# Second-product pairs moved beside the last column tiles of the first product in a fused encoder's feed-forward blocks

## The chip, the cores and the metric

The kernel runs on one core of one Trainium2 chip, as one launch. The metric is the device time of one execution in microseconds (us); lower is better. All times below are of that core.

## The reference

Two layers, each with a feed-forward block, a mixer (two kinds of attention) and a second feed-forward block, on 256 tokens of width 1024, all in float32:

```python
for l in range(DEPTH):                                   # DEPTH = 2
    x = layer_norm(ALPHA * x + 0.5 * swiglu(x, ffn1_w_in[l], ffn1_w_out[l]), ...)
    mix = hybrid_mixer(x, ...)
    x = layer_norm(ALPHA * x + mix, ...)
    x = layer_norm(ALPHA * x + 0.5 * swiglu(x, ffn2_w_in[l], ffn2_w_out[l]), ...)

def swiglu(x, w_in, w_out):                              # w_in 1024 x 5632, w_out 2816 x 1024
    gate, up = split(x @ w_in)
    return (silu(gate) * up) @ w_out
```

The mixer is untouched by the change; the four feed-forward blocks are all changed in the same way. They are called here by layer and place: 00, 02, 10, 12 (12 is the last).

## The kernel before, in words

Every float32 operand is split into a rounded high half (type fp32r) and the rest, and a product is three fp32r products. So each 128-row piece of a weight matrix is loaded by SyncE into a `raw` tile (128x1024, 512 KB; five buffers), ScalarE casts it into a high half `wh` (L118, for pairs L72), and VectorE subtracts to get the low half `wl` (L119, for pairs L73). `wh` and `wl` have nine buffers each. TensorE's order is the order of the code; the order on the other engines is set by a scheduler with priorities when the program is built (weight work has a low one), and each engine then runs its list strictly in that order.

A feed-forward block has 22 column tiles of the hidden width (index j, 128 wide). Tiles 0 to 3 are made by `first`. For tile 4 on, `col` makes for a tile two accumulations, `hg` (gate) and `hu` (up), each in one of the eight PSUM banks: eight matmuls of 512 columns with `wh` (L419, `wide`) and eight of 256 with `wl` (L424, `narrow`). `col` takes two tiles j, j+1 at a time (the first two singly), so four banks are in use and the other four rest; the order of wide and narrow alternates (`flip`). ScalarE then copies half of a bank to `tl` (L434), VectorE adds the other half (L435), ScalarE applies Silu (L436), VectorE multiplies (L438), and the result is split into high and low halves in a tile `g` (L441, L442). A g tile holds two column tiles, so its index is q = j/2.

The second product multiplies g (22 pieces of 128 of the inner dimension, index k) with `w_out`. A single piece ("o", `step`, L503) costs 12 matmuls of 512 columns for the two token halves t = 0, 1. Six couples of pieces (q = 3 to 8, the tuple STR) use a Strassen-like scheme instead (`pair`, L527): seven products of three matmuls, 21 where two singles take 24. For this VectorE makes four sums of blocks of g (`sums`, L457 to L460, with their halves at L461 and L462) and four sums of blocks of the two raw weight pieces (`_make_pair`, L86 to L89), whose halves come out as three full `wh`/`wl` tiles and one half tile `t4` (index b, t, a, f in the tile names). Lookahead for weights is counted in slots, nine in all; a pair counts four.

The order in a block: all 22 column tiles; then, by PLAN, `o o S o S S S S S` (o a single, S a pair); then the pair accumulators in four extra banks (`pp`) are folded into x by VectorE (L540 to L549); then seven more singles (TAIL) for t = 0, layer norm of t = 0, the same seven for t = 1 with the transposes of the normed t = 0 (`to_xt`, L327) put three half-steps ahead of the end, and layer norm of t = 1. Norm weights (`lng`, `lnb`) have a tile each of their own and are loaded in `col`'s loop.

Of the kernel before, what the change touches and what calls it, by code (L numbers as in the profile page):

```python
# [33 lines left out]
TAIL = 7  # L34
# [6 lines left out]
STR = (3, 4, 5, 6, 7, 8)  # L41
PLAN = "o o S o S S S S S"
# [17 lines left out]
class Weights:  # L60
# [6 lines left out]
    def _halves(self, i, raw, nm=""):  # L67
        nc = self.nc
        n = raw.shape[-1]
        wh = self.pool.tile([P, 1024], F32R, tag="wh", name=f"wh{i}{nm}", bufs=9)  # L70
        wl = self.pool.tile([P, 1024], F32R, tag="wl", name=f"wl{i}{nm}", bufs=9)
        nc.scalar.copy(wh[:, 0:n], raw)  # L72
        nc.vector.tensor_tensor(wl[:, 0:n], raw, wh[:, 0:n].bitcast(F32), ALU.subtract)  # L73
        return [tuple(w[:, c : c + 512] for w in (wh, wl)) for c in range(0, n, 512)]
# [21 lines left out]
    def _slots(self, i):  # L96
        return 4 if self.srcs[i][0] == "S" else 1

    def _make(self, i):
# [4 lines left out]
        wh = self.pool.tile([P, 1024], F32R, tag="wh", name=f"wh{i}", bufs=9)  # L104
        wl = self.pool.tile([P, 1024], F32R, tag="wl", name=f"wl{i}", bufs=9)
# [30 lines left out]
def encoder_kernel(  # L136
# [36 lines left out]

    singles = [k for k in range(JT) if k // 2 not in STR]
    singles, tail = singles[: len(singles) - TAIL], singles[len(singles) - TAIL :]
    plan, left, pairs = [], list(singles), list(STR)
    for u in PLAN.split():
        plan.append((u, (left if u == "o" else pairs).pop(0)))
    assert not left and not pairs

    def out_rows(w):
        row = lambda k: w[k * P : (k + 1) * P, :]
        rows = [row(k) if u == "o" else ("S", row(2 * k), row(2 * k + 1)) for u, k in plan]
        return rows + [row(k) for k in tail]

    srcs = []
    for l in range(DEPTH):
        srcs += [f1_b[l, k] for k in range(KT)]
        srcs += [f1_in[l, j, s] for j in range(JT - NB) for s in range(2)]
        srcs += out_rows(f1_out[l])  # L190
# [8 lines left out]
        srcs += [f2_b[l, k] for k in range(KT)]  # L199
        srcs += [f2_in[l, j, s] for j in range(JT - NB) for s in range(2)]  # L200
        srcs += out_rows(f2_out[l])
# [111 lines left out]
    def load_gb(l, n):  # L313
        gt = wp.tile([P, D], F32, tag="lng", name=f"lng{l}{n}")
        nc.sync.dma_start(gt, ln_g[l, n].partition_broadcast(P))
        bt = wp.tile([P, D], F32, tag="lnb", name=f"lnb{l}{n}")
        nc.sync.dma_start(bt, ln_b[l, n].partition_broadcast(P))
        return gt, bt
# [42 lines left out]
    def ffn(l, n, last=False):  # L361
        nonlocal wi
        nm = f"{l}{n}"
        gs = [gp.tile([P, 2, 2, SEQ], F32R, tag="g", name=f"g_{nm}_{q}") for q in range(JT // 2)]
# [29 lines left out]
        def first_t(gv, t):  # L394
# [3 lines left out]
            for q in range(2):  # L398
                a = slice(t * P, (t + 1) * P)
                dh = gs[q][:, :, 0, a]  # L400
                nc.scalar.copy(dh, tr[:, 2 * q : 2 * q + 2, :])
                dv.tensor_tensor(gs[q][:, :, 1, a], tr[:, 2 * q : 2 * q + 2, :], dh.bitcast(F32), ALU.subtract)

        def col(*js, flip=False):
# [3 lines left out]
            for j in js:  # L408

                hs = [ps.tile([P, 2, SEQ], F32, tag="b", name=f"h{'gu'[s]}_{nm}_{j}") for s in range(2)]  # L410
                tl = tp.tile([P, 2, SEQ], F32, tag="tl", name=f"tl_{nm}_{j}", bufs=2)
# [3 lines left out]

            def wide(hs, ws, s):
                for k in range(KT):

                    mm(hs[s], ws[s][0][:, k * P : (k + 1) * P], xx[:, k], start=(k == 0 and not flip),  # L419
                       stop=(k == KT - 1 and flip), skip_group_check=flip)  # L420

            def narrow(hs, ws, s):
                for k in range(KT):
                    mm(hs[s][:, 1, :], ws[s][1][:, k * P : (k + 1) * P], xx[:, k, 0], start=(k == 0 and flip),  # L424
                       stop=(k == KT - 1 and not flip), skip_group_check=flip)

            one, two = (narrow, wide) if flip else (wide, narrow)
            for j, hs, tl, ws in ts:
                for s in range(2):
                    one(hs, ws, s)  # L430
            for j, hs, tl, ws in ts:
                for s in range(2):
                    two(hs, ws, s)
                    nc.scalar.copy(tl[:, s], hs[s][:, 1, :])  # L434
                    dv.tensor_tensor(tl[:, s], hs[s][:, 0, :], tl[:, s], ALU.add)  # L435
                nc.scalar.activation(tl[:, 0], tl[:, 0], AF.Silu)  # L436
                gv = tl[:, 1]
                dv.tensor_tensor(gv, tl[:, 0], gv, ALU.mult)  # L438
                q, jj = divmod(j, 2)
                n = P if q in STR and jj == 0 else SEQ  # L440
                nc.scalar.copy(gs[q][:, jj, 0, 0:n], gv[:, 0:n])  # L441
                dv.tensor_tensor(gs[q][:, jj, 1, 0:n], gv[:, 0:n], gs[q][:, jj, 0, 0:n].bitcast(F32), ALU.subtract)  # L442
                if q in STR and jj:
                    sums(q, ts[0][2][:, 1], gv)

        sm = {}

        def sums(q, g0, g1):

            f = tp.tile([P, 4, P], F32, tag="tmp", name=f"sf_{nm}_{q}")  # L450
            if STR.index(q) < 3:
                s = xp.tile([P, 2, 4, P], F32R, tag="x", name=f"s_{nm}_{q}")
                sh, sl = s[:, 0], s[:, 1]
            else:
                sh, sl = (tp.tile([P, 4, P], F32R, tag="tmp", name=f"s{c}_{nm}_{q}") for c in "hl")
# [22 lines left out]
        for j in (NB + 1, *range(NB + 2, JT, 2)):  # L478

            col(*((j,) if j == NB + 1 else (j, j + 1)), flip=(j % 4 == 0 or j == NB + 1))  # L480
# [3 lines left out]
            if j == JT - 6:  # L484
                gb = load_gb(l, n)
                if n == 0:
                    load_mix(l)

        k0, k1 = singles[0], tail[-1]
        kl = tail[-SPLIT]  # L490
        acc = [[(slice(512 * h, 512 * h + 512), ps.tile([P, 512], F32, tag="b", name=f"acc_{nm}_{t}{h}"),
                 k0, tail[-SPLIT - 1] if last and t and h else k1) for h in range(2)] for t in range(2)]
# [12 lines left out]
        pp = {}  # L505

        def pair(q, w, first, final):
            b11, b21, b22, t4, t1, t2, t3 = w
            if first:
                for c in (5, 7, 1, 6):  # L510
                    pp[c] = ps.tile([P, 512], F32, tag="b", name=f"pp_{nm}_{c}")
            sh, sl = sm[q]
            blk = lambda kk, t: [gs[q][:, kk, e, t * P : (t + 1) * P] for e in range(2)]
            smb = lambda c: (sh[:, c], sl[:, c])
            s1, s2, s3, s4 = (smb(c) for c in range(4))
            for o, (ah, al), (bh, bl) in (
                (acc[0][0][1], blk(1, 0), b21),
                (acc[0][1][1], s4, b22),
                (pp[5], s1, t1),
                (pp[7], s3, t3),  # L520
                (pp[1], blk(0, 0), b11),
                (pp[6], s2, t2),
                (acc[1][0][1], blk(1, 1), t4),
            ):
                own = any(o is p for p in pp.values())
                for e, (g, ww) in enumerate(((ah, bh), (ah, bl), (al, bh))):
                    mm(o, g, ww, start=(own and first and e == 0), stop=(own and final and e == 2))  # L527

# [453 lines left out]
```

## Time and profile before

| | us |
|---|---|
| median of 3 runs (lowest, highest) | 929.22 (928.66, 930.1) |
| the profiled execution, its own time | 929.28 |
| its span, first to last instruction | 927.5 |
| TensorE busy in the span | 919.1 |
| VectorE busy | 804.9 |
| ScalarE busy | 577.8 |
| block 10 from start to end (463.1 to 643.0) | 179.9 |

In profile rows PE is TensorE's matmuls, PEld its weight loads, DVE VectorE, ACT ScalarE, POOL GpSimd, SPq SyncE's queue, and L12 is line 12 of the kernel. A busy TensorE says little by itself, since matmuls overlap and their ends are modelled: what counts is the spacing of their starts. For VectorE and ScalarE too, a row's duration is longer than the spacing of two such instructions behind one another. A timeline row merges neighbours of one kind; its figures are start and duration, and in brackets stands how long the engine idled ahead of it and what ended that.

### The profile page before, as it was taken

To read this page: it belongs to the slowest core of one execution; us is meant where nothing else is said; L and a number is where in the kernel's file an instruction comes from. 1 tells how busy PE (TensorE), PEld (TensorE's weight loads), DVE (VectorE), ACT (ScalarE), POOL (GpSimd) and SP (SyncE) were. 2 spreads that over 40 slices of the span, in tenths; PEclk is the share of its full clock that TensorE was granted. 3 is DMA by queue.
4 is the path that set the end of the run, shared out by engine and by line. 5 is a ranking of instruction groups with operands and counts; after the bars stand their busy time and mean duration, and the time that the engine had idled before them with its cause. 6 is when DMAs were issued, how large, how long until landed. Compare 5 with 4: busy or idle time off the path is not lost.

```text
span 927.5 us, 13795 instructions
## 1 busy us (share of the span) xinstructions
PE 919.1 (99%) x4958; PEld 784.9 (85%) x4958; DVE 804.9 (87%) x1388; ACT 577.8 (62%) x982; POOL 17.0 (2%) x27
## 2 busy tenths in 40 slices
PE   9999999999999999999999999999999999999996
PEld 6888888888878888888888888888888888888885
DVE  7898899998987677899986888999988876888997
ACT  5768656546865666656646666664478656666660
POOL 0000000000000000000000000000000000000000
PEclk9999999999999999999999999999999999999998
DMA  8976445774426755545775665466844365665451
GB/s 320 313 265 203 160 137 191 246 260 154 128 90 206 248 182 182 159 136 191 257 262 196 187 192 168 136 231 208 290 112 137 100 236 188 189 192 163 136 205 46
DMA packets 51380, 176.30 MB, mean 190 GB/s; under 512 B 6512, under 2 KB 8304, under 8 KB 51312
## 3 DMA queue, kind: packets, MB, share of 16 engines
q1 hardware_dynamic: 51024, 175.03, 58.0%
q8 instruction: 39, 0.64, 0.3%
q10 hardware_dynamic: 288, 0.39, 0.1%
q14 instruction: 29, 0.24, 0.1%
HBM read 174.35 MB, written 1.05 MB: 189 GB/s over the span
## 4 chain that ended last, share of the span: by engine, by line
PE 98%; DMA 1%; DVE 1%; SPq 0%; issue 0%; ACT 0%; DVEq 0%
PE hg L419 14%; PE hu L419 14%; PE acc L503 12%; PE hb L381 9%; PE hu L424 7%; PE hg L424 7%; PE pp L527 7%; PE acc L527 5%; PE ao L840 5%; PE os L776 1%; PE pj_sq L617 1%; PE pj_sq L619 1%; PE pj_dv L617 1%; PE pj_sq L618 1%; PE pj_dq L618 1%; PE pj_dv L619 1%
## 5 line engine op out<-in xcount | busy, mean ns | idle before, releaser
L119 DVE TENSOR_TENSOR wl<-raw,wh 128x1024 fp32r<-128x1024 f32 (+1 forms) x271 | 325.2, 1207 | 57.0 <-PE hg L424 20.2
L118 ACT CAST wh<-raw 128x1024 fp32r<-128x1024 f32 (+1 forms) x271 | 282.1, 1046 | 99.7 <-PE acc L503 14.8
L419 PE MATMUL hg<-xx,wh 128*128 128x512 f32 x576 | 143.1, 390 | 0.0
L419 PE MATMUL hu<-xx,wh 128*128 128x512 f32 x576 | 142.3, 389 | 0.0
L419 PEld LDWEIGHTS hu<-xx,wh 128*128 128x128 f32 x576 | 108.1, 188 | 22.5
L419 PEld LDWEIGHTS hg<-xx,wh 128*128 128x128 f32 x576 | 106.6, 188 | 21.2
L503 PE MATMUL acc<-wh,g 128*128 128x512 f32 (+1 forms) x326 | 90.5, 386 | 0.0
L424 PE MATMUL hg<-xx,wl 128*128 128x256 f32 x576 | 81.0, 283 | 0.0
L424 PE MATMUL hu<-xx,wl 128*128 128x256 f32 x576 | 80.9, 283 | 0.0
L424 PEld LDWEIGHTS hg<-xx,wl 128*128 128x128 f32 x576 | 75.4, 191 | 1.6
L424 PEld LDWEIGHTS hu<-xx,wl 128*128 128x128 f32 x576 | 74.3, 192 | 0.0
L503 PEld LDWEIGHTS acc<-wh,g 128*128 128x128 f32 x326 | 60.9, 188 | 12.2
L381 PE MATMUL hb<-wh,xx 128*128 128x512 f32 x256 | 69.5, 391 | 0.4 <-ACT wh L118 0.4
L381 PEld LDWEIGHTS hb<-wh,xx 128*128 128x128 f32 x256 | 47.7, 188 | 11.3 <-ACT wh L118 1.6
L503 PE MATMUL acc<-wl,g 128*128 128x512 f32 (+1 forms) x163 | 51.7, 385 | 0.0
L434 ACT COPY tl<-hg 128x256 f32<-128x256 f32 x72 | 26.7, 371 | 30.9 <-PE hg L419 27.4
L434 ACT COPY tl<-hu 128x256 f32<-128x256 f32 x72 | 26.9, 373 | 19.6 <-PE hu L424 16.8
L381 PE MATMUL hb<-wl,xx 128*128 128x512 f32 x128 | 38.9, 390 | 0.0
L441 ACT CAST g<-tl 128x128 fp32r<-128x128 f32 (+1 forms) x72 | 26.7, 371 | 19.2 <-DVE tl L438 18.2
L840 PE MATMUL ao<-wh,xx 128*128 128x512 f32 x128 | 37.0, 398 | 0.0
L503 PEld LDWEIGHTS acc<-wl,g 128*128 128x128 f32 x163 | 30.6, 188 | 6.1
L436 ACT ACTIVATE tl<-tl 128x256 f32<-128x256 f32 x72 | 30.1, 418 | 6.5 <-DVE tl L435 5.7
(1140 smaller groups left out, 1576.3 us busy)
## 6 DMA issues: line engine op xcount, KB each, us to landing
raw<-in_f_in_dram SPq DMA_DIRECT2D x144, 512.0 KB, 4.4
raw<-in_f_out_dram SPq DMA_DIRECT2D x40, 512.0 KB, 4.5
raw<-in_m_in_dram SPq DMA_DIRECT2D x36, 512.0 KB, 4.4
raw<-in_f_b_dram SPq DMA_DIRECT2D x29, 512.0 KB, 4.3
raw<-in_m_out_dram SPq DMA_DIRECT2D x8, 512.0 KB, 5.0
raw<-in_m_out_dram SPq DMA_DIRECT2D x16, 256.0 KB, 4.4
lng<-in_ln_g_dram SPq DMA_DIRECT2D x6, 512.0 KB, 4.9
lnb<-in_ln_b_dram SPq DMA_DIRECT2D x6, 512.0 KB, 6.2
```

What stands on the lines that cost most here:

```text
L118: nc.scalar.copy(wh[:, s], raw[:, s])
L119: nc.vector.tensor_tensor(wl[:, s], raw[:, s], wh[:, s].bitcast(F32), ALU.subtract)
L381: mm(hb[s], xx[:, k, g, t, :], ww[:, 512 * s : 512 * s + 512], start=(k == 0 and e == 0), stop=(k == KT - 1 and e == 2))
L419: mm(hs[s], ws[s][0][:, k * P : (k + 1) * P], xx[:, k], start=(k == 0 and not flip), stop=(k == KT - 1 and flip), skip_group_check=flip)
L424: mm(hs[s][:, 1, :], ws[s][1][:, k * P : (k + 1) * P], xx[:, k, 0], start=(k == 0 and flip), stop=(k == KT - 1 and not flip), skip_group_c ...
L434: nc.scalar.copy(tl[:, s], hs[s][:, 1, :])
L436: nc.scalar.activation(tl[:, 0], tl[:, 0], AF.Silu)
L441: nc.scalar.copy(gs[q][:, jj, 0, 0:n], gv[:, 0:n])
L503: mm(a, g, ww[:, s], start=(k == ka and e == 0), stop=(k == kb and e == 2))
L527: mm(o, g, ww, start=(own and first and e == 0), stop=(own and final and e == 2))
L617: mm(o, xx[:, k, 0, t, :], wh[:, s], start=(k == 0), stop=False)
L840: mm(acc[t][h], xx[:, k, g, t, :], ww[:, s], start=(k == 0 and e == 0), stop=(k == KT - 1 and e == 2))
```

## The change

- STR becomes (2, ..., 9): eight pairs, no singles among them, and a TAIL of six singles (k = 0, 1, 2, 3, 20, 21). PLAN is gone.
- The pairs no longer follow the column tiles. Column tiles 4 to 13 are made as before; tiles 14 to 21 (MIX = 14) are made one half at a time, and pair i stands beside tile 14+i: three of its seven products, half `hg`, the other four products, half `hu`. All seven products have a bank of their own (`pp`), the four that were summed into output banks before too; the halves `hg` and `hu` of tiles 14 to 21 share the eighth.
- For these halves, ScalarE copies the whole bank (128x512) to `hc` at high priority, and VectorE adds its two halves from there.
- Weights are loaded in the new order, and a pair counts three slots, since its half tile `t4` has two buffers of its own.
- The norm weights lie in the pool of g, which gives the memory for that, and are loaded behind tile 19. The high and low halves of `sums` for q = 5 to 9 lie there too.

```diff
-TAIL = 7
+TAIL = 6
-STR = (3, 4, 5, 6, 7, 8)
-PLAN = "o o S o S S S S S"
+STR = (2, 3, 4, 5, 6, 7, 8, 9)
+MIX = 14
     def _halves(self, i, raw, nm=""):
...
+        tag, bufs = ("", LOOK + 1) if n == 1024 else ("f", 2)
+        wh = self.pool.tile([P, n], F32R, tag="wh" + tag, name=f"wh{i}{nm}", bufs=bufs)
...
-        return 4 if self.srcs[i][0] == "S" else 1
+        return 3 if self.srcs[i][0] == "S" else 1
...
+        for j in range(NB, JT):
+            if j >= MIX and j - MIX < len(STR):
+                q = STR[j - MIX]
+                rows.append(("S", row(2 * q), row(2 * q + 1)))
+            rows += [w_in[j - NB, 0], w_in[j - NB, 1]]
         return rows + [row(k) for k in tail]
...
-        gt = wp.tile([P, D], F32, tag="lng", name=f"lng{l}{n}")
+        gt = gp.tile([P, D], F32, tag="g", name=f"lng{l}{n}")
...
+        def half(j, s, tl):
+            nonlocal wi
+            h, w = bank(j, s), W.get(wi)
+            wi += 1
+            wide(h, w)
+            narrow(h, w)
+            with tc.high_priority():
+                hc = tp.tile([P, 2, SEQ], F32, tag="tmp", name=f"hc_{nm}_{j}{s}")
+                nc.scalar.copy(hc, h)
+            dv.tensor_tensor(tl[:, s], hc[:, 0], hc[:, 1], ALU.add)
...
+        def pair(i, w):
...
+            todo = ((2, blk(1, 0), b21), (3, s4, b22), (5, s1, t1), (7, s3, t3),
+                    (1, blk(0, 0), b11), (6, s2, t2), (4, blk(1, 1), t4))
+            for m, (c, (ah, al), (bh, bl)) in enumerate(todo):
+                if c not in pp:
+                    pp[c] = ps.tile([P, 512], F32, tag="b", name=f"pp_{nm}_{c}")
+                if m == 3:
+                    yield
+                for e, (g, ww) in enumerate(((ah, bh), (ah, bl), (al, bh))):
+                    mm(pp[c], g, ww, start=(i == 0 and e == 0), ...)
+            yield
+
+        for j in range(MIX, JT):
+            tl = tl_tile(j)
+            if j - MIX < len(STR):
+                w = W.get(wi)
+                wi += 1
+                run = pair(j - MIX, w)
+            for s in range(2):
+                if j - MIX < len(STR):
+                    next(run)
+                half(j, s, tl)
+            gated(j, tl)
+            loads(j)
```

`gated` is what `col` did from Silu on, `bank` allocates a bank.

ScalarE, block 10, column tiles 14 and 15, as the list stood before: `hg` and `hu` are banks of column tiles, `tl` takes their half, `wh187` is the high half of weight piece 187.

```order
L434 COPY tl_10_14_5680<-hg_10_14_5678 128x256
L434 COPY tl_10_14_5680<-hu_10_14_5679 128x256
L436 ACTIVATE tl_10_14_5680<-tl_10_14_5680 128x256
L434 COPY tl_10_15_5695<-hg_10_15_5693 128x256
L434 COPY tl_10_15_5695<-hu_10_15_5694 128x256
L441 CAST g_10_7_4903<-tl_10_14_5680 128x128
L436 ACTIVATE tl_10_15_5695<-tl_10_15_5695 128x256
L441 CAST g_10_7_4903<-tl_10_15_5695 128x256
L461 CAST sh_10_7_5789<-sf_10_7_5788 128x512
```

The same place in the list of the change, from the copy of `hg` of tile 15 to that of tile 16; `wh179b`, `wh179t`, `wh179a`, `wh179f` are the halves of the pair that is used beside tile 17, `wh180` and `wh181` those of tile 17's own weights.

```order
L448 COPY hc_10_150_5950<-hg_10_15_5927 128x512
L73 CAST wh179b_5976<-raw179b_5967 128x1024
L422 ACTIVATE tl_10_15_5911<-tl_10_15_5911 128x256
L73 CAST wh179t_5980<-raw179t_5968 128x1024
L73 CAST wh179a_5984<-raw179a_5966 128x1024
L119 CAST wh180_6025<-raw180_6024 128x1024
L448 COPY hc_10_151_6008<-hu_10_15_5965 128x512
L73 CAST wh179f_5988<-t4_179_5971 128x512
L119 CAST wh181_6041<-raw181_6040 128x1024
L429 CAST g_10_7_5908<-tl_10_15_5911 128x256
L448 COPY hc_10_160_6062<-hg_10_16_6039 128x512
```

The casts of a pair and of a column tile's weights now stand between the two copies that empty the bank, where before the copies of a tile stood side by side.

VectorE, block 10, from the last addition of tile 13 to the first of tile 14, in the list of the change:

```order
L419 TENSOR_TENSOR tl_10_13_5683<-hu_10_13_5682,tl_10_13_5683 128x256
L74 TENSOR_TENSOR wl173a_5703<-raw173a_5684,wh173a_5702 128x1024
L424 TENSOR_TENSOR tl_10_13_5683<-tl_10_13_5683 128x256
L74 TENSOR_TENSOR wl173f_5707<-t4_173_5689,wh173f_5706 128x512
L430 TENSOR_TENSOR g_10_6_5764<-tl_10_13_5683,g_10_6_5764 128x256
L479 TENSOR_TENSOR sf_10_6_5791<-tl_10_12_5674,tl_10_13_5683 128x128
L120 TENSOR_TENSOR wl174_5802<-raw174_5800,wh174_5801 128x1024
L480 TENSOR_TENSOR sf_10_6_5791<-tl_10_12_5674,sf_10_6_5791 128x128
L120 TENSOR_TENSOR wl175_5822<-raw175_5820,wh175_5821 128x1024
L482 TENSOR_TENSOR sf_10_6_5791<-tl_10_13_5683,sf_10_6_5791 128x128
L449 TENSOR_TENSOR tl_10_14_5799<-hc_10_140_5842 128x256
L87 TENSOR_TENSOR raw176t_5863<-raw176a_5861 128x512
```

And the list before, from the same instruction on:

```order
L435 TENSOR_TENSOR tl_10_13_5576<-hu_10_13_5575,tl_10_13_5576 128x256
L119 TENSOR_TENSOR wl182_5683<-raw182_5681,wh182_5682 128x1024
L438 TENSOR_TENSOR tl_10_13_5576<-tl_10_13_5576 128x256
L457 TENSOR_TENSOR sf_10_6_5669<-tl_10_12_5561,tl_10_13_5576 128x128
L458 TENSOR_TENSOR sf_10_6_5669<-tl_10_12_5561,sf_10_6_5669 128x128
L442 TENSOR_TENSOR g_10_6_4902<-tl_10_13_5576,g_10_6_4902 128x256
L460 TENSOR_TENSOR sf_10_6_5669<-tl_10_13_5576,sf_10_6_5669 128x128
L462 TENSOR_TENSOR sl_10_6_5671<-sf_10_6_5669,sh_10_6_5670 128x512
L119 TENSOR_TENSOR wl183_5689<-raw183_5687,wh183_5688 128x1024
L435 TENSOR_TENSOR tl_10_14_5680<-hg_10_14_5678,tl_10_14_5680 128x256
```

What moved: the pairs' weight work, which stood behind the last column tile, now stands between the additions of column tiles 10 to 20.

164 lines of the change are left out of this document (74 added, 90 removed).

## Prediction

> **What bounds the kernel now.** I read the page's shares first, then the chain of work that ended last, then the windows of one block.
>
> ```profile
> span 927.5 us, 13795 instructions
> PE 919.1 (99%) x4958; PEld 784.9 (85%) x4958; DVE 804.9 (87%) x1388; ACT 577.8 (62%) x982; POOL 17.0 (2%) x27
> PE 98%; DMA 1%; DVE 1%; SPq 0%; issue 0%; ACT 0%; DVEq 0%
> ```
>
> The chain runs through TensorE for 98% of the span, and VectorE, at 87%, is the next that could bind. Whether TensorE really issues without gaps is read from its timeline: one late stretch of pairs, then wide and narrow groups of column tiles.
>
> ```profile
> 439.62 0.39 PE L527 MATMUL pp<-wh138t,sh 128*128 128x512 f32 x1
> ...
> 442.34 0.39 PE L527 MATMUL acc<-wh138f,g 128*128 128x512 f32 x1
> ...
> 442.79 0.39 PE L527 MATMUL acc<-wh138f,g 128*128 128x512 f32 x1
> 348.85 1.12 PE L424 MATMUL hg<-xx,wl 128*128 128x256 f32 x8
> 349.81 1.12 PE L424 MATMUL hu<-xx,wl 128*128 128x256 f32 x8
> ...
> 358.26 1.98 PE L419 MATMUL hg<-xx,wh 128*128 128x512 f32 x8
> 360.07 1.98 PE L419 MATMUL hu<-xx,wh 128*128 128x512 f32 x8
> ```
>
> From 439.62 to 442.79 are 14 starts: 0.2264 us for a matmul of 512 columns. Eight wide ones take 1.81, eight narrow ones 0.96. There is no bracket of idleness in any row. So a removed matmul is worth 0.2264 us, as long as TensorE still waits for nothing. The windows show where that is close:
>
> ```profile
> 416.70:443.20 26.50, 26.50 (x118) 21.95 (x117) 25.88 (x30) 16.65 (x20) 0.00 (x0) 1.00 0.60 200
> 339.85:362.05 22.20, 22.20 (x129) 19.68 (x129) 17.70 (x35) 14.70 (x27) 0.00 (x0) 1.00 0.64 190
> ```
>
> The columns are length, then busy time of PE, PEld, DVE, ACT and POOL, the granted clock, the DMA share and GB/s. In the pair stretch (first row) VectorE is busy 25.88 of 26.50 us; beside four column tiles (second row) 17.70 of 22.20.
>
> **The change part by part.**
>
> *Matmuls.* Two more pairs per block replace four singles: 2 x (24 - 21) = 6 matmuls fewer, 24 in four blocks. 24 x 0.2264 = 5.43 us, all on the path. The rest of TensorE's work is only reordered.
>
> *VectorE's load beside tiles 14 to 21.* One pair's weight work, from its first row to that of the next:
>
> ```profile
> 425.19 0.68 DVE L86 TENSOR_TENSOR raw137t<-raw137a 128x512 f32<-128x512 f32 x1
> 425.80 0.68 DVE L87 TENSOR_TENSOR raw137t<-raw137a,raw137b 128x512 f32<-128x512 f32 x1
> 426.40 1.21 DVE L73 TENSOR_TENSOR wl137b<-raw137b,wh137b 128x1024 fp32r<-128x1024 f32 x1
> 427.53 0.68 DVE L88 TENSOR_TENSOR raw137a<-raw137b,raw137t 128x512 f32<-128x512 f32 x1
> 428.13 1.21 DVE L73 TENSOR_TENSOR wl137t<-raw137t,wh137t 128x1024 fp32r<-128x1024 f32 x1
> 429.27 0.68 DVE L89 TENSOR_TENSOR t<-raw137b,raw137a 128x512 f32<-128x512 f32 x1
> ...
> 431.61 0.68 DVE L86 TENSOR_TENSOR raw138t<-raw138a 128x512 f32<-128x512 f32 x1
> ...
> 395.60 0.41 DVE L438 TENSOR_TENSOR tl<-tl 128x256 f32<-128x256 f32 x1
> 395.94 0.41 DVE L435 TENSOR_TENSOR tl<-hg,tl 128x256 f32<-128x256 f32 x1
> ...
> 352.60 0.28 DVE L459 TENSOR_TENSOR sf<-tl 128x128 f32<-128x128 f32 x1
> 352.80 0.28 DVE L457 TENSOR_TENSOR sf<-tl,tl 128x128 f32<-128x128 f32 x1
> ```
>
> By their starts a pair costs 6.42 us, a row of 1024 elements 1.14, of 512 0.60, of 256 0.34, of 128 0.20. Two steps (two column tiles and two pairs beside them) ask VectorE for 2 x 6.42 + 4 x 1.14 for the column weights + 7 x 0.34 + 0.20 for additions, products and low halves + 4 x 0.20 + 0.60 for one `sums` = 21.4 us. TensorE's step is 21 x 0.2264 + 2 x (1.81 + 0.96) = 10.29, two are 20.6. So VectorE falls behind by 0.8 us in two steps. Before, the same pair work (6.42 against 21 x 0.2264 = 4.75) overran more, but it was hidden: TensorE used the last tile of pair 138 at 442.34, and VectorE made it here:
>
> ```profile
> 437.43 0.68 DVE L73 TENSOR_TENSOR wl138f<-t,wh138f 128x512 fp32r<-128x512 f32 x1
> ```
>
> That is a lead of 4.2 us at the end, and no bank depended on it.
>
> *The one bank.* Seven banks hold the products, so a half may start only when ScalarE has copied the half before it. The copy stands in ScalarE's list behind the casts of the pair's `t` and `a` tiles and one more cast; the cast of `a` waits for VectorE's third sum (L88 before, L89 now). So the bank now hangs on VectorE's weight work. The nearest rows for ScalarE:
>
> ```profile
> L736 ACT COPY pTs<-tps 128x512 f32<-128x512 f32 x16 | 8.4, 601 | 7.9 <-PE tps L734 7.9
> L795 ACT ACT_TABLE_LOAD x2 | 2.6, 1283 | 0.0
> ...
> 406.77 1.05 ACT L72 CAST wh134t<-raw134t 128x1024 fp32r<-128x1024 f32 x1
> 437.00 2.00 ACT L118 CAST wh<-raw 128x1024 fp32r<-128x1024 f32 x2
> 349.05 0.37 ACT L434 COPY tl<-hu 128x256 f32<-128x256 f32 x1 [0.53 <-PE hu L424]
> ```
>
> The copy is 0.6 us (L736), a cast 1.05 or 1.0 behind another, and ScalarE starts 0.2 us after the next group's first matmul (348.85 to 349.05). From the end of half `hg` of an odd tile: copy until 0.8, VectorE's addition 1.14, the first two sums (L87, L88) 2.34, the split of `b` 3.5, the third sum 4.1, cast `a` 5.15, next cast 6.15, copy of `hu` 6.75. TensorE wants the bank 2.72 (twelve pair matmuls) + 2.77 (half `hu`) + 2.04 (nine of the next pair) = 7.53 after it: 0.8 us to spare. In even tiles the low half of a `sums` (0.60) stands in VectorE's chain too: 0.2 to spare.
>
> *The first of these waits, tile 14 to 15.* Tile 13's last addition cannot come before tile 13's end, T. It starts at T + 0.6, and the nine rows behind it (three of 1024, one of 512, two of 256, three of 128) end at T + 6.2, while the copy of `hg` of tile 14 ends at T + 4.81 + 0.8 = T + 5.6. VectorE is 0.6 late, and the `sums` row is in the chain: 0.4 us of TensorE's time. Besides, VectorE may come late to T: from tile 9's last addition to tile 13's its list holds 21.8 us of work by the spacings above, for 22.2. Before, it idled 22.20 - 17.70 = 4.5 us there. If none of that idling stays, it is on time; if all, it is 4.1 late; with half, as I take it since half of the waits are for column banks that come as before, 1.8. First wait: 2.2 us, between 0.4 and 4.5.
>
> *The later ones.* Behind an odd tile 0.8 to spare takes VectorE's 0.4 per step; behind an even one (16 to 17, 18 to 19) the 0.2 does not cover 0.4 and the rest of the lag: 0.75 us each, between 0 and 1.5. From tile 20 on no pair is prepared, and the wait goes. Per block: 2.2 + 1.5 = 3.7, four blocks 14.8; block 00 also has the rotary tables in that stretch (23.5 us of work for 22.2): 1.7 more. 16.5 in all.
>
> *The tail.* t = 1 has 27 matmuls ahead of the transposes of normed t = 0 instead of 33, 6.1 us instead of 7.5, and before there was nothing to spare:
>
> ```profile
> 453.18 1.28 DVE L343 SCALAR_TENSOR_TENSOR x<-acc,x 128x512 f32<-128x512 f32 x2
> ...
> 458.76 1.41 DVE L355 SCALAR_TENSOR_TENSOR x<-x,rs,lnb 128x512 f32<-128x512 f32 x2
> 460.02 1.03 PE L327 MATMUL tr_y<-ident,x 128*128 128x128 f32 x8
> ```
>
> t = 0 ended at 460.02 - 7.47 = 452.55, its first normed half at 458.76 + 0.7 = 459.46, which is 6.9 later: 0.8 us of waiting in each of the three blocks that have it, 2.4, between 0 and 4.5 (nearly two rows of weight work more or none in that chain).
>
> *At nothing:* the weights' bytes are the same, only their order differs; the norm weights are loaded behind tile 19 and are wanted two tiles and a tail (over 20 us) later; the larger copies (0.6 for 0.37) lie in an engine 62% busy; three table loads (1283 ns each, L795) now stand in ScalarE's list beside tiles 20 and 21 of block 00, where no pair is cast. If that cover is gone, they cost up to 3.9 us, once; the norm weights, up to a landing.
>
> Sum on the profiled execution: 929.28 - 5.43 + 16.5 + 2.4 = 942.75. Its own 929.28 is the runs' median (929.22) to 0.01%, so nothing is corrected. About 0.2%, 1.9 us, is what a measurement can tell from no change.
>
> **The rivals.**
>
> *Everything stays hidden: 923.9, faster.* Place: the copy of `hu` at each step. It holds if VectorE reaches T on time and ScalarE's copy starts within 1.4 us of each half's end (2.04 - 0.6). For it: no row of TensorE before shows a wait, though VectorE had 25.88 of 26.50 us of work; the spare of odd tiles. Against: 21.4 us of work for 20.6. 929.28 - 5.43 = 923.85.
>
> *Raw tiles land late.* A pair's raw tiles reuse buffers of the pair before, so a load starts only when those are split.
>
> ```profile
> raw<-in_f_out_dram SPq DMA_DIRECT2D x40, 512.0 KB, 4.5
> 922.00:927.50 5.50, 0.00 (x0) 0.00 (x0) 2.50 (x5) 0.00 (x0) 0.79 (x1) 0.56 0.27 95
> ```
>
> Landing takes 4.5 us; VectorE's rows between the split of `t` and the next pair's L87 take some 6.5. Only if landing rose to 8.4 would it add 1.9 in each of six prepared steps, 45.6 in four blocks: 988. Against: 2 MB in 10.3 us is 204 GB/s, about the 200 of the pair stretch.
>
> *The clock falls in the waits.* The last row is the only one with TensorE idle for long; its granted clock is 0.56, against 1.00 in the windows quoted first. If each of 12 waits of 0.75 to 2.2 us (three per block) were followed by a first part (2.04 us) at 0.56, each would add 1.6, 19 in all: 962. [...]
>
> **How the numbers follow.** The forecast (waits at the one bank, slower) gets 0.64, of which 0.05 lies within 0.2% of 929.28, where its waits are at their low bounds but the first; everything hidden 0.23, nearly all of it over 0.2% faster; late raw tiles 0.05; the clock 0.08. The terms' lower ends give 4 x 0.4 - 5.43 = 925.4, the upper ones 929.28 - 5.43 + 4 x 7.5 + 1.7 + 4.5 = 960. The range, 923.5 to 959, also takes in the hidden case and leaves out the two dear rivals, 0.13. Faster 0.21, same 0.05, slower 0.74.
>
> **What would show it.** Right: TensorE's timeline has brackets ahead of the wide group of `hg` of tiles 15, 17 and 19, released by ScalarE's `hc`; ScalarE's `hc` of `hu` starts late, behind the cast of `a`; VectorE has hardly any idle time from tile 13 to 19; a wait of about 0.8 ahead of `tr_y`. Wrong in size: gaps at other tiles, or waits for `raw`. Wrong: no brackets there at all, and 24 matmuls less is the whole difference.

## The result and the profile after

The changed kernel takes 940.96 us (median of 4 runs, 940.01 to 941.37) against 929.14 (928.66 to 930.1) for the one before: ratio 1.0124, 95% interval 1.0107 to 1.0142. The forecast was 942.75. The profiled execution took 940.01, its span is 938.2, 10.7 us more than before.

The page's first lines and its chain of work that ended last, of the kernel after:

```profile
span 938.2 us, 13857 instructions
PE 919.4 (98%) x4934; PEld 779.5 (83%) x4934; DVE 844.6 (90%) x1476; ACT 593.1 (63%) x1003; POOL 17.0 (2%) x27
PE 60%; DVE 16%; issue 2%; ACT 1%; DMA 1%; DVEq 0%; ACTq 0%; SPq 0%
```

TensorE's count is down by the 24 matmuls and its busy time is the same, yet the chain that was 98% TensorE now runs through VectorE for 16%. VectorE has 39.7 us more to do (844.6 for 804.9). TensorE's waits by releaser (total, times, longest):

```profile
PE hg L409 <- ACT hc L448: 9.9, 12, 3.3
PE tr_y L325 <- DVE x L353: 0.7, 1, 0.7
```

Twelve waits for ScalarE's copy of the bank, three in each of the four blocks. TensorE's timeline shows where (start, time of the group, and in brackets the idle time before it with its releaser):

```profile
556.44 1.98 PE L409 MATMUL hu<-xx,wh 128*128 128x512 f32 x8
...
562.72 2.11 PE L409 MATMUL hg<-xx,wh 128*128 128x512 f32 x8 [1.28 <-ACT hc L448]
...
568.37 1.98 PE L409 MATMUL hu<-xx,wh 128*128 128x512 f32 x8
...
573.20 1.98 PE L409 MATMUL hg<-xx,wh 128*128 128x512 f32 x8
...
578.71 1.98 PE L409 MATMUL hu<-xx,wh 128*128 128x512 f32 x8
...
584.06 2.11 PE L409 MATMUL hg<-xx,wh 128*128 128x512 f32 x8 [0.35 <-ACT hc L448]
...
605.40 2.11 PE L409 MATMUL hg<-xx,wh 128*128 128x512 f32 x8 [0.35 <-ACT hc L448]
```

The rows are block 10: `hu` of tile 14, then `hg` of tiles 15, 17 and 19 behind a wait. The bracket is not the whole loss, since a group's end is modelled. Start to start shows it better. From `hu` to the next `hg` without a wait are 4.83 us (568.37 to 573.20), from `hg` to `hu` 5.51: a step is 10.34, two are 20.68. The two periods with a wait (562.72, 584.06, 605.40) are 21.34 each. So a later wait costs 0.66, and the first one 562.72 - 556.44 - 4.83 and 0.14 for the slower restart (568.37 - 562.72 is 5.65, not 5.51): 1.59. In the same way the first waits of blocks 00, 02 and 12 are 3.57, 1.71 and 1.52. Together 8.4 for the first waits, 8 x 0.66 = 5.3 for the later ones: 13.7 us.

What could pace the 21.34 is seen in the window of those two periods (length, busy time of PE, PEld, DVE, ACT, POOL; clock, DMA share, GB/s):

```profile
562.72:605.40 42.68, 41.98 (x213) 35.28 (x213) 42.68 (x67) 29.84 (x43) 0.00 (x0) 1.00 0.61 198
```

VectorE is busy for all of the 42.68 us; ScalarE is not (29.84); the granted clock is 1.00. This makes VectorE the suspect but does not prove it, since its rows last longer than they are spaced (two of 1.22 us in block 02, at 370.82 and 372.15, have their next row 1.13 and 1.14 us later): a run below shows it just as full with no wait of TensorE. And the list of ScalarE ahead of the first wait, in order of time:

```profile
560.19 1.06 ACT L73 CAST wh176a<-raw176a 128x1024 fp32r<-128x1024 f32 x1 [0.68 <-DVE raw176a L89]
561.15 1.03 ACT L119 CAST wh<-raw 128x1024 fp32r<-128x1024 f32 x1
562.09 0.57 ACT L448 COPY hc<-hu 128x512 f32<-128x512 f32 x1
```

Half `hu` of tile 14 ended at about 559.2 (its narrow group started at 558.25). The copy that frees the bank starts at 562.09, behind a cast that waited 0.68 for VectorE's third sum (L89) and behind one more cast.

At the end of the blocks, the transposes ahead of the mixer, block 00:

```profile
186.02 0.66 PE L325 MATMUL tr_y<-ident,x 128*128 128x128 f32 x4
187.39 0.66 PE L325 MATMUL tr_y<-ident,x 128*128 128x128 f32 x4 [0.71 <-DVE x L353]
```

They came in one go of 1.07 us before (to the next matmul); here it is 1.78, and 0.06 more ahead of them: 0.77 lost. In blocks 02 and 10 it is 1.21 for a group of 1.03: 0.18 each. The tail costs 1.1.

### The profile page after: what moved, and what is told of

Read it like the earlier page. It is cut to its first block, busy times and chain, and to the rows that moved or that the text cites. A ratio compares the mean times of both kernels' runs of the same rounds, so it can differ in the third digit from the quotient of the medians.

```text
span 938.2 us, 13857 instructions
## 1 busy us (share of the span) xinstructions
PE 919.4 (98%) x4934; PEld 779.5 (83%) x4934; DVE 844.6 (90%) x1476; ACT 593.1 (63%) x1003; POOL 17.0 (2%) x27
## 3 DMA queue, kind: packets, MB, share of 16 engines
HBM read 174.35 MB, written 1.05 MB: 187 GB/s over the span
## 4 chain that ended last, share of the span: by engine, by line
PE 60%; DVE 16%; issue 2%; ACT 1%; DMA 1%; DVEq 0%; ACTq 0%; SPq 0%
PE hg L409 7%; PE hu L409 7%; PE hb L382 7%; PE ao L869 5%; PE pp L534 4%; PE pp L565 4%; PE hg L414 4%; PE hu L414 4%; DVE wl L120 2%; PE acc L565 1%; DVE tl L449 1%; PE os L805 1%; PE pj_sq L646 1%; PE pj_sq L648 1%; DVE t L90 1%
## 5 line engine op out<-in xcount | busy, mean ns | idle before, releaser
L120 DVE TENSOR_TENSOR wl<-raw,wh 128x1024 fp32r<-128x1024 f32 (+1 forms) x255 | 305.6, 1207 | 36.0 <-ACT wh L119 23.0
L119 ACT CAST wh<-raw 128x1024 fp32r<-128x1024 f32 (+1 forms) x255 | 264.2, 1044 | 91.8 <-PE acc L565 20.6
L414 PEld LDWEIGHTS hu<-xx,wl 128*128 128x128 f32 x576 | 76.2, 191 | 2.5
L565 PE MATMUL pp<-wh,g 128*128 128x512 f32 x144 | 43.1, 390 | 0.0
L448 ACT COPY hc<-hg 128x512 f32<-128x512 f32 x32 | 18.7, 585 | 30.4 <-PE hg L414 30.4
L483 ACT CAST s<-sf 128x512 fp32r<-128x512 f32 x32 | 19.8, 619 | 21.2 <-DVE sf L482 21.2
L565 PEld LDWEIGHTS pp<-wh,g 128*128 128x128 f32 x144 | 26.8, 188 | 5.4
L424 DVE TENSOR_TENSOR tl<-tl 128x256 f32<-128x256 f32 x72 | 30.2, 420 | 0.3
L449 DVE TENSOR_TENSOR tl<-hc 128x256 f32<-128x256 f32 x64 | 26.8, 419 | 4.0 <-ACT hc L448 4.0
```

The costliest lines, as they stand in the source:

```text
L119: nc.scalar.copy(wh[:, s], raw[:, s])
L120: nc.vector.tensor_tensor(wl[:, s], raw[:, s], wh[:, s].bitcast(F32), ALU.subtract)
L414: mm(h[:, 1, :], w[1][:, k * P : (k + 1) * P], xx[:, k, 0], start=(k == 0 and flip), stop=(k == KT - 1 and not flip), skip_group_check=flip)
L449: dv.tensor_tensor(tl[:, s], hc[:, 0], hc[:, 1], ALU.add)
L565: mm(a, g, ww[:, s], start=(k == ka and e == 0), stop=(k == kb and e == 2))
```

## The experiments

The waits have a place (the bank, through ScalarE's list) and, by the prediction, a source (VectorE's 21.4 us of work for TensorE's 20.6). The runs take away or change one of the two at a time, but the scheduler sorts every run's lists anew, so the order on ScalarE and VectorE shifts in places too. Ratios are to the kernel before, with 95% intervals; the changed kernel's is 1.0124.

**Two banks.** In the pair's products:

```diff
+                a4 = c == 4
+                c = 2 if a4 else c
...
-        acc = [[(lo, pp[2], ...)], [(lo, pp[4], None, tail[-1]), ...
+        c21 = ps.tile([P, 512], F32, tag="b", name=f"acc_{nm}_10")
+        acc = [[(lo, pp[2], ...)], [(lo, c21, tail[0], tail[-1]), ...
```

> The fourth of the seven sums goes into the bank of the second instead of a bank of its own, so the halves of tiles 14 to 21 have two banks in turn; the sums of the first columns of both token tiles are wrong by that, and the last steps of that quarter start a new bank. Matmuls, casts, additions and DMAs are as many as in the changed kernel. Theory (one shared bank: a half cannot start until ScalarE has copied the half before, and that copy stands behind a cast that waits for VectorE): the waits before hg of tiles 15, 17 and 19 go, about 8.4 us of first waits and 4 x 2 x 0.66 = 5.3 us of later ones, so 940.5 - 13.7 = 927, range 925 to 930. Rival (VectorE makes the pairs' halves more slowly than TensorE uses them, and the bank only shows it): the same time is lost before a product of a pair, waiting for its weights, 936 to 941.

Measured: 935.37 us, 1.0066 (1.0051 to 1.0081). Neither theory has it: the waits at the bank are gone, and only 5.6 of the 13.7 us came back. TensorE's waits and one place in its timeline:

```profile
PE tr_y L325 <- DVE x L353: 4.2, 5, 1.9
PE pp L536 <- DVE s L484: 1.2, 1, 1.2
PE pp L536 <- ACT s L483: 1.1, 1, 1.1
```

```profile
464.04 0.66 PE L325 MATMUL tr_y<-ident,x 128*128 128x128 f32 x4 [1.92 <-DVE x L353]
465.30 0.92 PE L325 MATMUL tr_y<-ident,x 128*128 128x128 f32 x4 [0.60 <-DVE x L353]
465.88 0.77 PE L568 MATMUL acc<-wh,g 128*128 128x512 f32 x1
466.45 0.63 PE L568 MATMUL acc<-wl,g 128*128 128x512 f32 x1
466.88 1.05 PE L568 MATMUL acc<-wh,g 128*128 128x512 f32 x2
```

TensorE runs ahead, and the same lag of VectorE is paid where TensorE next needs something of VectorE's: the last pair's `sums` in block 00, the layer norm's output ahead of the transposes in 00, 02 and 10. So the bank is a place of the wait more than its source. The matmuls behind the second wait start 0.57 and 0.43 us apart, not 0.23, which goes with a granted clock of 0.72 from 464 to 470 (last section): nine of them take 3.58 us for 2.04, so 1.5 of the 8 us still lost are the clock's.

**More work for VectorE.**

```diff
+            dv.tensor_tensor(hc[:, 0], hc[:, 0], hc[:, 0], ALU.max)
             dv.tensor_tensor(tl[:, s], hc[:, 0], hc[:, 1], ALU.add)
```

> One more VectorE operation of 128x256 per half in tiles 14 to 21 (the maximum of the copy's first half with itself, 0.335 us), so 1.34 us per two steps. Theory (VectorE, at 21.34 us per two steps against TensorE's 20.68, sets the pace): each of the two later periods of a block grows by the whole 1.34 and the first wait by 0.7 to 1.3, perhaps another 1.3 at tile 21: 4 x (2.7 + 0.7 to 2.6) = 13.5 to 21 us more, 954 to 961. Rival (the place of the copy in ScalarE's queue or the landing of raw weights sets the waits, VectorE has room): 941 to 943.

Measured: 963.41 us, 1.0369 (1.0353 to 1.0384). Two of the later waits of block 10:

```profile
596.80 2.12 PE L409 MATMUL hg<-xx,wh 128*128 128x512 f32 x8 [1.46 <-ACT hc L448]
619.48 2.11 PE L409 MATMUL hg<-xx,wh 128*128 128x512 f32 x8 [1.47 <-ACT hc L448]
```

The period is 22.68 = 21.34 + 1.34: all of the added VectorE time, to the hundredth, is in TensorE's step. The total is 2 us above the theory's range, because the transposes now wait too (6.8 us in six waits, 0.7 in the changed kernel). ScalarE's copy of `hu` stands at the same place of its list, behind the cast of `a` and one more; the rival falls.

**Less work for VectorE.** Two runs leave out low halves of the pairs' weights:

```diff
-        wl = self.pool.tile([P, n], F32R, tag="wl" + tag, ...)
...
-        nc.vector.tensor_tensor(wl, raw, wh.bitcast(F32), ALU.subtract)
+        if nm in ('f',):          # second run: ('f', 'a')
+            wl = wh
+        else:
+            wl = self.pool.tile([P, n], F32R, tag="wl" + tag, ...)
+            nc.vector.tensor_tensor(wl, raw, wh.bitcast(F32), ALU.subtract)
```

> The half tile of each pair's weights (t4) has no low half: TensorE takes the high half twice, so its products lose their low part, and VectorE has one 128x512 subtraction less per pair (0.6 us, 1.2 per two steps, so about 20.15 us against TensorE's 20.68). Everything else is as in the changed kernel. Theory, narrowed by the two-bank run (VectorE's backlog is paid, before the bank or, if the bank is not there, before sums and transposes): the two later waits of each block go (5.3 us), the first ones shrink by about 1.2 each (two pairs made before them), and the late transposes by about 1: 940.5 - 5.3 - 4.8 - 1 = 929.4, range 926 to 932. Rival (the copy's place or the cover of a wait by three products sets it, whatever VectorE does): 936 to 941.

> As the run before, and the last full tile of each pair (b11 and t2) has no low half either: VectorE has 0.6 + 1.135 = 1.74 us less per pair, 3.47 per two steps, so 17.9 us. Theory (VectorE's backlog): all waits at the bank and before the transposes go, 940.5 - 13.7 - 1.1 = 925.7, range 924 to 928. Rival (place or cover): 936 to 941.

Measured: 931.48 us, 1.0018 (1.0007 to 1.0028), and 926.28, 0.9956 (0.9940 to 0.9973); the second is faster than the kernel before. All of TensorE's waits for the bank, of the first and of the second of these:

```profile
PE hg L412 <- ACT hc L451: 3.9, 1, 3.9
```

```profile
PE hg L412 <- ACT hc L451: 0.2, 1, 0.2
```

There is still one bank, and ScalarE's copy of `hu` still stands behind the cast of `a` and one more (in the second run behind the cast of `f` too). The waits are gone with VectorE's load, but for one in block 00 that needed the second step. Four steps of block 10 in the first of these runs:

```profile
557.60:599.05 41.45, 41.45 (x213) 35.36 (x213) 41.45 (x65) 30.89 (x44) 0.00 (x0) 1.00 0.65 208
```

TensorE's steps are 10.35 to 10.41 here, without a bracket, and VectorE still shows no idle time, though by the spacings it has 20.14 us of work in two steps (21.34 - 1.2) for TensorE's 20.68. With the run before, this settles the source of the later waits: VectorE's work per step, not the place of the copy. For the first waits it is less clean, because VectorE's third sum also stands earlier in the newly sorted list; how much of their fall is load and how much is order is not shown. By block (the shift of the same matmul against the kernel before, from one stage to the next), the second run saves 0.84, 0.90, 0.87 and 1.05 us, where 6 matmuls are 1.36. The rest goes where pair matmuls and column groups alternate: a step is 10.34 by its rows, not 10.29 as added up from its parts, and 8 x 0.05 is 0.4 per block.

**The other split of a pair.**

```diff
-                if m == 3:
+                if m == 4:
```

> The first half of a pair that stands ahead of a column half is four products (2.72 us) and the second three (2.04 us), the other way round from the changed kernel; work and order on VectorE are the same. Theory (VectorE's pace): the waits move to other places and the sum stays, 939 to 942. Rival (three products are too short a cover for the copy of the bank): the 0.68 us more of cover takes that much from each of the 12 waits, 940.5 - 8.2 = 932, range 931 to 936.

Measured: 944.57 us, 1.0155 (1.0133 to 1.0176), some 3 us more than the changed kernel and 2.6 above the theory's upper end, and nowhere near the rival. The first waits of blocks 02, 10 and 12 fell by about 0.7 (brackets of 1.40, 1.28 and 1.22 became 0.70, 0.51 and 0.48), the later ones kept 0.34, and more than that came back at the transposes:

```profile
PE hg L409 <- ACT hc L448: 7.6, 12, 3.3
PE tr_y L325 <- DVE x L353: 5.3, 5, 1.7
```

The waits at the bank fell by 2.3 us, those at the transposes rose by 4.6. Besides, the granted clock fell to 0.59 behind block 00's first wait, which it did not in the changed kernel's profile (1.00):

```profile
100.25 3.17 PE L409 MATMUL hg<-xx,wh 128*128 128x512 f32 x8 [3.29 <-ACT hc L448]
```

To the next group are 2.97 us, not 1.95, and the narrow group behind takes 1.49, not 0.95: some 1.6 of the 5.0 us between the two profiled spans (943.2 and 938.2). More cover moves a wait; it does not take it away while VectorE is the slower one.

**Seven pairs.**

```diff
-TAIL = 6
-STR = (2, 3, 4, 5, 6, 7, 8, 9)
+TAIL = 8
+STR = (2, 3, 4, 5, 6, 7, 8)
```

> Seven pairs in tiles 14 to 20 and eight single tiles at the end: 12 matmuls more than the changed kernel (2.7 us). Theory (VectorE's backlog, built up in every mixed step from the first on): the first wait and that of tile 17 are as before, that of tile 19 and the late transposes lose up to 0.7 each in four blocks: 940.5 + 2.7 - 0 to 4 = 941, range 939 to 943.5. Rival (the two additional pairs as such overload the columns): half of the 13.7 us of waits go with one of the two, 934 to 938.

Measured: 951.59 us, 1.0233 (1.0218 to 1.0249). Both expectations miss. Tile 21 has no pair now, and its two halves follow one another on the one bank with nothing between:

```profile
633.30 2.12 PE L409 MATMUL hg<-xx,wh 128*128 128x512 f32 x8 [0.68 <-ACT hc L448]
637.08 2.12 PE L409 MATMUL hu<-xx,wh 128*128 128x512 f32 x8 [0.72 <-ACT hc L448]
```

From `hg` to `hu` are 3.78 us for 2.77 of work (1.81 + 0.96), 1.0 lost, and from tile 20's `hu`, which starts at 629.70, to this `hg` 3.60, 0.8 lost: 1.8 per block, 7 in all; block 00's first wait also grew, to 5.28. Here the bank itself is the source: with no pair between, its turnaround costs 1 us. Neither theory had thought of that, so the run says nothing on how VectorE's backlog scales with the number of pairs.

**Work handed to GpSimd.** Two runs, the additions and the last cast of a pair:

```diff
-            dv.tensor_tensor(tl[:, s], hc[:, 0], hc[:, 1], ALU.add)
+            nc.gpsimd.tensor_tensor(tl[:, s], hc[:, 0], hc[:, 1], ALU.add)
```

```diff
-        nc.scalar.copy(wh, raw)
+        (nc.gpsimd.tensor_copy if eng else nc.scalar.copy)(wh, raw)
...
-            b11, t2 = self._halves(i, r0, "a")
+            b11, t2 = self._halves(i, r0, "a", 1)
```

> The two additions of a copied half's two parts per step go to GpSimd, so VectorE has 4 x 0.335 = 1.34 us less per two steps, 20.0 against TensorE's 20.68. Theory (VectorE's pace): the later waits go (5.3 us), the first ones shrink by 0.7 to 1.3 each: 940.5 - 5.3 - 2.8 to 5.3 = 930 to 932.5, range 928 to 935. Rival (ScalarE's order alone): the waits stay, 939 to 942. Second rival (GpSimd slows VectorE, or its slower addition makes the gate late): 941 or more.

> The last full cast of a pair (the one ScalarE waits in for VectorE, with the copy of the bank behind it) goes to GpSimd; VectorE's work is unchanged at 21.34 us per two steps. Theory in its narrow form (the waits come because the copy stands in order behind that cast): the copy is early, the bank is free, and VectorE's lag of 0.66 us per two steps, 2.7 per block, is taken up by the weights made ahead: 927 to 931. Rival (VectorE's pace sets the end whatever the order): the waits move to the pair's weights or stay, 936 to 941. If GpSimd's cast takes several us, or slows VectorE, its halves are late: over 941.

Measured: 978.48 us, 1.0535 (1.0513 to 1.0558), and 969.30, 1.0430 (1.0412 to 1.0447). Both are far over, by the last case of each expectation. Of the first run, the group of GpSimd's additions, then one place on GpSimd, VectorE and ScalarE:

```profile
L449 POOL TENSOR_TENSOR tl<-hc 128x256 f32<-128x256 f32 x64 | 109.6, 1712 | 584.8 <-ACT hc L448 470.7 <-DVE sf L482 80.5 <-DVE wl L120 19.7
```

```profile
583.79 0.84 POOL L449 TENSOR_TENSOR tl<-hc 128x256 f32<-128x256 f32 x1 [4.92 <-ACT hc L448]
```

```profile
583.95 1.76 DVE L74 TENSOR_TENSOR wl176a<-raw176a,wh176a 128x1024 fp32r<-128x1024 f32 x1
```

```profile
578.90 0.42 ACT L422 ACTIVATE tl<-tl 128x256 f32<-128x256 f32 x1 [1.88 <-POOL tl L449]
```

An addition that takes 0.335 us of VectorE's time takes 1.71 here on average; the VectorE row above, 1.22 us long elsewhere, took 1.76 behind one; and ScalarE, in order, waits 1.88 for the sum of the gate half with everything behind it, the next copy of the bank too (34.1 us of TensorE's waits for it, 9.9 in the changed kernel). The cast on GpSimd took 2.76 and 2.97 us in two places of block 10 (1.05 on ScalarE), and VectorE's low half waited for it. So these two do not test VectorE's relief. They show that a slower engine ahead of an in-order list is paid like VectorE's lag.

**The rotary tables early.**

```diff
         if first_x:
+            rotary()
             g0, g1 = first((0, 1))
...
                 load_x()
-                rotary()
```

> The changed kernel with the rotary tables (some 31 short VectorE operations of about 0.2 us) written at the start of block 00, where VectorE still idles, and not at tile 6; nothing else is moved by hand. Theory (VectorE's backlog): only block 00 gains, its first wait falls from 3.57 to the 1.5 to 1.7 of the other blocks: 940.7 - 2 = 939, range 938 to 940. Rival (block 00's wait is longer for another reason, such as raw weights that land late): 940.5 to 941.5. If VectorE has no room at the start either: over 941.5.

Measured: 941.49 us, 1.0132 (1.0113 to 1.0150): nothing gained, which is in the rival's range. Block 00's first wait is a bracket of 4.72, not the 3.27 of the changed kernel. ScalarE's list ahead of it:

```profile
92.64 1.05 ACT L73 CAST wh34b<-raw34b 128x1024 fp32r<-128x1024 f32 x1 [3.40 <-DMA raw34b<-in_f_out_dram]
```

The cast of the third pair waits 3.40 us for a raw tile, whose DMA could be issued only when VectorE had freed a tile (at 87.4, with 5.2 to land). VectorE itself then idles for a cast that ScalarE has behind this one:

```profile
94.24 0.69 DVE L484 TENSOR_TENSOR s<-sf,s 128x512 fp32r<-128x512 f32 x1 [1.21 <-ACT s L483]
```

So the late landing, the rival's mechanism, hides whatever the early tables gained. Whether the tables are worth the 1.7 us that the prediction gave them is not shown.

**Six raw tiles.**

```diff
-    gp = ctx.enter_context(tc.tile_pool(name="gp", bufs=11))
+    gp = ctx.enter_context(tc.tile_pool(name="gp", bufs=10))
...
-    ... tag="raw", name=f"raw{i}{c}", bufs=5
+    ... tag="raw", name=f"raw{i}{c}", bufs=6
```

> The changed kernel with six raw tiles for the weights and not five (a tile of g's pool is given up for it, ten and not eleven). Ahead of the first wait ScalarE stood 1.16, 2.24 and 2.0 us in blocks 00, 02 and 12 for a raw tile of the third pair that landed late, its DMA having been issued only when VectorE had freed a raw tile. Theory (VectorE's backlog: the raw tile is late because VectorE is, and VectorE's work stays the same): an earlier landing only moves the wait, 939 to 941.5. Rival (the landing itself is the cause of the first waits): they shrink by about those 5.4 us, 935.5, range 934 to 937.5. If the pool of g is now short: over 942.

Measured: 939.52 us, 1.0105 (1.0088 to 1.0122). The theory's range holds it. What became of the wait for the landing, on ScalarE:

```profile
89.45 1.06 ACT L73 CAST wh34b<-raw34b 128x1024 fp32r<-128x1024 f32 x1
...
94.92 1.05 ACT L73 CAST wh34t<-raw34t 128x1024 fp32r<-128x1024 f32 x1 [3.57 <-DVE raw34t L88]
```

The raw tile is there 3.4 us earlier, its cast does not wait, and the next cast in the list waits 3.57 us for VectorE instead. So the late landing was for the most part a sign of VectorE's lag. A smaller part was its own: the earlier landing was worth 0.3 to 0.5 us in each of blocks 02, 10 and 12 (their brackets fell from 1.40, 1.28 and 1.22 to 0.91). The changed kernel, block 02, from the end of tile 13 to the first addition of tile 14:

```profile
366.62 0.39 PE L534 MATMUL pp<-wh112b,g 128*128 128x512 f32 x1
...
367.88 0.42 DVE L419 TENSOR_TENSOR tl<-hu,tl 128x256 f32<-128x256 f32 x1
...
372.44 1.05 ACT L73 CAST wh118b<-raw118b 128x1024 fp32r<-128x1024 f32 x1 [2.24 <-DMA raw118b<-in_f_out_dram]
...
374.00 0.42 DVE L449 TENSOR_TENSOR tl<-hc 128x256 f32<-128x256 f32 x1 [0.43 <-ACT hc L448]
```

The cast waits for the landing, the copy of `hg` stands behind the cast, and VectorE idles 0.43 us for the copy (0.30 and 0.22 in blocks 10 and 12); with six raw tiles it does not idle there. The gain may be larger than the time shows, because the granted clock fell to 0.61 in block 00 of the profiled execution (99 to 103), which cost some 1.6 us: the wide and the narrow group behind the wait took 4.47, not 2.90. The one execution with a mean granted clock of 0.998 (the others have 0.995) took 938.2, between the two ranges.

**A version that gives TensorE VectorE's addition.** In tiles 14 to 21 each half accumulates its three parts into the same 256 columns, gate and up half in the two halves of the one bank:

```diff
+            for k in range(KT):
+                for e in range(2):
+                    mm(h, w[0][:, k * P : (k + 1) * P], xx[:, k, e], start=(k == 0 and e == 0), stop=False)
+            for k in range(KT):
+                mm(h, w[1][:, k * P : (k + 1) * P], xx[:, k, 0], start=False, stop=(k == KT - 1))
+            if s:
+                nc.scalar.copy(tl[:, 1], h)
+            else:
+                nc.scalar.activation(tl[:, 0], h, AF.Silu)
```

> Each half of tiles 14 to 21 is three runs of 256 columns into the same 256 columns, not one of 512 and one of 256: TensorE adds the parts, VectorE's addition goes (0.67 us per step) and ScalarE reads the gate's Silu straight from the bank; gate and up half have each their half of the bank. The output is the reference's. TensorE's price by the spacing of the rows (3 x 0.96 us against 1.81 + 0.96): 0.11 x 64 = 7.0 us. Theory (VectorE's backlog): VectorE at 20.0 us per two steps against TensorE's 21.1, waits go but for block 00's 2 us and 0.6 per block as in the run without the half tile's low part: 929.3 - 5.4 + 7.0 + 2.4 + 2 = 935, range 932 to 938. Rival (no backlog is saved, TensorE's extra work just adds): 944 to 948.

> The run before and the early rotary tables together. Theory: both gains add, 933, range 930 to 936: better than the changed kernel, not than the one before. Rival (once the backlog is small the tables' place no longer matters): as the run before, 934 to 937.

Measured: 933.72 us, 1.0045 (1.0027 to 1.0063), and with the early tables 934.87, 1.0055 (1.0036 to 1.0074). The window of block 10's mixed steps in the first of the two:

```profile
566.00:604.00 38.00, 38.00 (x249) 34.85 (x248) 37.65 (x57) 25.18 (x38) 0.00 (x0) 1.00 0.64 208
```

TensorE does not idle at all there; in block 00 three waits of 1.0 us in all are left. 7 us of additional matmuls buy 13.7 us of waits: 7.2 us better than the changed kernel, and still 4.5 behind the one before. The two column halves also have a half of the bank each, so this run does not by itself tell VectorE's load from the bank. The early tables again bring nothing. No version here with the reference's output beats the kernel before.

## Why the prediction was right, step by step

- **24 matmuls, 5.43 us.** The count is right. The step that failed is "all on the path. The rest of TensorE's work is only reordered": 0.4 per block, 1.6 in all, goes where pairs and columns alternate (10.34 for 10.29).
- **VectorE's load.** 21.4 against 20.6 was forecast; 21.34 and 20.68 are measured. The run with 1.34 us more gave 22.68, and those with less lost the later waits. Shown.
- **The one bank through ScalarE's list.** The places are right (tiles 15, 17, 19; the copy behind the cast of `a` and one more). As a source it was taken too far: with a second bank 8 of the 13.7 us were still paid, 1.5 of them by the clock.
- **First waits.** Forecast 2.2 each, measured 1.71, 1.59 and 1.52. That this is near is luck in part, since two sizes were wrong in opposite directions. The last addition of tile 13 starts 1.26 us after that tile's end in blocks 02, 10 and 12 (366.62 to 367.88 above), where the forecast had 0.6 for a VectorE on time. So VectorE came 0.66 late to it, not 1.8. And the copy of `hg` of tile 14 ended 7.2 to 7.4 us after the end of tile 13, not 5.6, behind a cast that had waited 2.0 to 2.2 us (in blocks 02 and 12 for the landing). The forecast had no such wait; it cost VectorE 0.2 to 0.4 us. In block 00 3.9 was forecast and 3.57 measured, but that 1.7 of it is the rotary tables' is not shown. Two limits lie close together there, VectorE's lag and the landing of the third pair's raw tile: ScalarE waited 3.40 us for the landing with the early tables and 3.63 with 0.6 us less work per pair, where the wait at the bank was still 3.92. With 1.74 less it was gone. What each of the two costs in block 00 stays open.
- **Later waits.** 0.75 forecast, 0.66 measured.
- **The tail.** 2.4 forecast, 1.1 measured, most of it in block 00. The chain was right, since it grew when VectorE's lag was not paid earlier (two banks 4.2, the other split 5.3) and when VectorE had more work (6.8). Its size was not; the two-bank run suggests why, since the waits at the bank give VectorE time to catch up before the tail.
- **Sum.** Forecast -5.43 + 16.5 + 2.4 = +13.5; by these rows -5.4 + 1.6 + 13.7 + 1.1 = +11.0, for a span longer by 10.7.
- **Rivals.** All hidden: no, but 926.28 with 1.74 us less per pair shows that its 923.9 was near what the change gives when VectorE keeps up. Late raw tiles: they were late before the first waits, mostly as a sign of the lag, with a price of their own of 0.3 to 0.5 us a block. The clock: 1.00 in a window of 4 us at each of the twelve waits of the changed kernel's profile, so none of its 10.7 us. But the other three executions have a mean granted clock of 0.996 for its 0.998 and took 0.7 to 1.4 us longer, so about 1 us of the median's 11.8 may be the clock's; they have no trace to show it.

## What to carry to other kernels

Here an engine that was not the bound was put at 103% of the bound's step, and the whole excess was paid, at whatever handover came first; another buffer or more cover there moved most of the wait to the next handover. So add up every engine's work for one step of the new order, as here from the spacings of the rows, before counting what the bound saves. To find the source of a wait, change the load of the suspected engine by a known time and see whether the period follows; to remove the place alone (two banks, six raw tiles, another split) showed mainly where it went next. A busy share of 100% does not find it, as the VectorE that was busy throughout those four steps without a wait of TensorE shows.

## What the runs showed of the hardware

**The clock fell behind a wait of 2.82 us and did not behind one of 3.27.** Granted clock (the figure before the last two) behind block 00's first wait, in the changed kernel (bracket 3.27) and with six raw tiles (bracket 2.82):

```profile
99.00:103.00 4.00, 3.32 (x18) 2.94 (x19) 4.00 (x7) 2.62 (x6) 0.00 (x0) 1.00 0.77 262
```

```profile
99.00:103.00 4.00, 3.83 (x12) 3.17 (x13) 4.00 (x7) 2.41 (x5) 0.00 (x0) 0.61 0.81 254
```

The shorter wait brought the clock down, the longer one did not. Every other bracket above 2 us at the bank, in all runs, was followed by a fall (granted clock of the 4 us from the group's start): 3.09 (0.65), 3.29 (0.59), 3.58 (0.61), 3.92 (0.59), 4.72 (0.57) and 5.28 (0.50) at block 00's first wait, and six of 2.42 to 4.60 with the additions on GpSimd (0.50 to 0.63). It also fell behind the two waits at the transposes with two banks (0.72 from 464 to 470). Of the brackets below 2 us at the bank two were followed by slow matmuls (1.82 and 1.83, with the cast on GpSimd), while another 1.83 and a 1.81 of the same run were not. In the changed kernel's trace eleven gaps of 0.34 to 1.40 us and one of 3.27 left the clock at 1.00.

**Where a GpSimd addition and a VectorE subtraction overlapped, one of the two took longer.** With the additions on GpSimd, take the addition that began at 583.79 and VectorE's subtraction that began at 583.95 (both above): the subtraction took 0.54 us longer, where 0.68 was left of the addition. Of the 77 such subtractions (L74, L120) that overlap an addition, 17 were longer, each by some 0.13 less than what was left. The other 60 kept their time, and there it was the addition that took longer:

```profile
117.12 4.89 POOL L449 TENSOR_TENSOR tl<-hc 128x256 f32<-128x256 f32 x1 [4.13 <-DVE wl L120]
```

This one had seven VectorE rows beside it, none longer than usual; with no VectorE row beside it an addition took 0.73 to 0.74 us.

**A group behind a wait restarted slower:** eight wide matmuls took 2.11 to 2.14 us, not 1.98, on each of the changed kernel's twelve waits. The second matmul started 0.34 us after the first, not 0.23, and the next group 0.14 later.
